# Two queue items per conv tile, and the value's weights requested as soon as the gate's unit runs

## The chip, the cores and the metric

The kernel runs on one core of one Trainium2 chip. The metric is the device time of one execution in microseconds; what is given is the median of several runs on one chip. The core has TensorE (PE in the profile, with its weight loads as PEld), VectorE (DVE), ScalarE (ACT), GpSimd (POOL) and SyncE (SP), which here only issues DMAs.

## The reference

Two layers run over 512 latent and 256 context tokens of width 1024. In each layer one input projection feeds three mixers, and a gated merge joins them; a gated feed-forward network follows.

```python
h = modulate(rms_norm(x)); a, na, qkv, og, dec, bet, mg = split(h @ w_in)
# A: a = [value | gate], 2 x 512 columns
y = value * sigmoid(gate); y = depthwise_conv31(y); ya = silu(layer_norm(y))
yb = neighbourhood_attention(norm(q), norm(k), v)        # from na, 3 x 512 columns
yc = gated_deltanet(qkv, dec, bet, og)                   # triangular solve per chunk, then a scan
x = x + m * (sum_b sigmoid(mg_b) * (y_b @ w_branch_b)) @ w_out
x = x + m' * conv_ffn(modulate(rms_norm(x)))
```

In the second layer the context tokens produce only keys and values, so their merge, feed-forward network and conv branch drop out.

## The kernel before

Every product with weights is done three times on split numbers: a weight tile of 128 x 1024 values arrives as `raw` by a DMA on SP's queue (L143, two buffers), ScalarE casts it to `whi` (L150, three buffers), VectorE takes the rest as `wlo` (L151, three buffers), and TensorE adds up whi x hi, whi x lo and wlo x hi. The function `wunit` does this for one tile.

The order of each engine's instructions is fixed before the run: the framework's scheduler places ready work, with the order of the program as its priority. Engines execute their own list strictly in order, and a buffer that is to be written again waits until its last reader is done.

The gated DeltaNet branch leaves TensorE much idle time: for each of two head pairs it builds a matrix E from decays, inverts its triangular blocks (`gdn_inverse`, whose off-diagonal 32 x 32 products write `iy`, `it` and `ir`, L986 to L999, after DMAs that gather `Td` and `E`), then scans the chunks, and ends in transposes `oT` (L933) copied to `oev` and stored. Between its steps the program calls `fill(us)`, which takes about that much TensorE work from `self.queue`, a queue of independent generators ("filler"). `fill` (L440 to L456) runs one generator at a time; when it starts one, it also advances the next one to its first yield, which is where the next one asks for its weights. So one item's weights are always requested one item ahead.

The queue holds, in this order: units of the neighbourhood attention's projection (`na_units`, L600 to L627: 36 units in layer 0 and 32 in layer 1; six units, or four, share one pair of weight tiles, which the first unit of such a set requests, so a set holds two of the three whi slots as long as it runs); among them the four conv tiles (`conv_a_proj`) at the places `CV_AT` gives; `na_finish`; and then 24 units of merge-gate projection (`mg_units`, L1036 to L1045), with the conv branch's layer norm between the last of them. A projection unit (`proj_gen`, L463 to L475) asks for its weights, yields, and then runs 24 matmuls per token stream: `pjl` for 512 latent tokens and, in layer 0, `pjc` for 256 context tokens. An na unit has 24 matmuls of 256 columns.

Places are `CV_AT = ((10, 12, 24, 36), (0, 10, 20, 30))`. In layer 0 sets have six units, so tile c0 stands inside the second set, c1 and c2 at the end of a set, and c3 behind the last. In layer 1 the sets have 4, 6, 6, 4, 6 and 6 units; c0 stands ahead of all, c1 and c2 at the end of a set, c3 inside the last.

A conv tile is one generator in the kernel before: gate projection, value projection, then tanh of the gate (ACT, L514), its product with the value (DVE, L515) and the store (L516). Only the gate's weights can be requested ahead; the value's are requested when the generator comes to its second `proj_gen`.

After the second head pair of a layer comes the attention (`attention`, L1055 and on): 12 loads of `ax` (10 in layer 1), transposes `aT` (L1071), loads of `vc` and `vl`, scores `sc` (L1121, L1122), the bias by DMA, row sums on VectorE (L1125), the normalised weights `P` (L1128) and their transposes `PT` (L1135). Beside this VectorE computes the conv branch's taps (L546). The rest of the filler is run up by a loop ahead of the merge (L434 to L437).

Of the kernel before, what the change touches and what calls it, by code (L numbers as in the profile page):

```python
# [9 lines left out]
F32 = mybir.dt.float32  # L10
F32R = mybir.dt.float32r
I32 = mybir.dt.int32
AF = mybir.ActivationFunctionType
ALU = mybir.AluOpType
# [50 lines left out]
class Net:  # L65
# [309 lines left out]
    def layer(self, l):  # L375
        nc, tc = self.nc, self.tc
        last = l == DEPTH - 1
        self.l, self.last = l, last
        dr = lambda n, sh: self.dr.tile(sh, F32, tag=n, name=n)
        self.d_ya, self.d_yc = dr("ya", [4, 128, NT]), dr("yc", [4, 128, NT])  # L380
        self.d_na = [dr(f"na{i}", [NT, 512]) for i in range(3)]
        self.d_sg, self.d_mg = dr("sg", [NT, 512]), dr("mg", [24, 128, NT])
        self.d_row = dr("row", [48, 128])
        self.d_ca, self.d_cy = dr("ca", [4, 128, NT]), dr("cy", [4, 128, NT])
        self.d_tok = {n: dr("tok" + n, [4, 128, 6, 128]) for n in "kv"}
        self.d_e = [dr(f"e{i}", [4, 24, 1024]) for i in range(3)]

        with ExitStack() as es:
            self.cp = es.enter_context(tc.tile_pool(name=f"cv{l}", bufs=1))
            with tc.tile_pool(name=f"head{l}", bufs=1) as self.hp:  # L390
                with tc.tile_pool(name=f"pre{l}", bufs=2) as self.ep:
                    self.km = self.hp.tile([128, 512], F32, name="km")
                    nc.sync.dma_start(self.km, self.A["km"])
                    self.og_proj()
                    self.gates()
                    self.gdn_proj()
                na, mg = self.na_units(), self.mg_units()
                cv = [self.conv_a_proj(i) for i in range(4)]
                ln = [self.conv_a_norm(t) for t in range(2 if last else 0, 6)]
                order = list(na)  # L400
                for i, p in enumerate(CV_AT[l]):
                    order.insert(i + p, cv[i])
                order.append(self.na_finish())
                for i, f in enumerate(mg):
                    order.append(f)
                    if len(mg) - i <= len(ln):
                        order.append(ln[len(ln) - len(mg) + i])
                self.queue = deque(order)
                self.live = None
                with tc.tile_pool(name=f"gdn{l}", bufs=1) as self.gp:  # L410
                    self.marks = []
                    for pr in range(2):
                        self.gdn_core(pr)
            while self.na_left:
                self.fill(0.1)
            taps = [f for c in range(4) for f in self.conv_a_taps(c)]
            self.open_zx()
            with tc.tile_pool(name=f"att{l}", bufs=2) as self.ap:
                self.attention(taps)
        with ExitStack() as es:  # L420
            if not last:
                self.dp = es.enter_context(tc.tile_pool(name="ada", bufs=2))
                self.ada_rows()
                self.todo = self.ada_steps(0, [*range(16, 24), *range(32, 40), *range(24, 32), *range(40, 48)]) + self.ada_steps(1, range(48))
            else:
                self.todo = []
            self.finish(l)
        if last:
            self.zes.close()
# [76 lines left out]

    def conv_a_proj(self, c):

        nc, l = self.nc, self.l
        ga = yield from self.proj_gen(self.A["w_b"][l, 4 + c], not self.last)  # L510
        aa = yield from self.proj_gen(self.A["w_b"][l, c], not self.last)
        for s, n in self.streams():
            th = self.tp.tile([128, 512], F32, tag="t1", name="th")
            nc.scalar.activation(th[:, :n], ga[s], AF.Tanh, scale=0.5)  # L514
            nc.vector.scalar_tensor_tensor(th[:, :n], th[:, :n], 1.0, aa[s], ALU.add, ALU.mult)  # L515
            nc.sync.dma_start(self.d_cy[c][:, self.sl(s)], th[:, :n])  # L516

    def conv_a_taps(self, c):

# [928 lines left out]
```

## Time and profile before

| | |
|---|---|
| median of three runs | 2603.09 us (2597.68 to 2608.0) |
| the profiled execution | 2592.68 us |
| its span | 2590.9 us |
| TensorE busy | 2495.3 us (96%) |
| VectorE busy | 1853.1 us (72%) |
| ScalarE busy | 1068.0 us (41%) |
| mean granted clock of TensorE | 0.983 |

The profile is one execution, with times from the start of its span. Waits are put down to the event that came last. Matmuls overlap in the array, so the cost of one in a run of them is read from start to start, not from the length that the row gives.

### The profile page before, as it was taken

To read this page: it belongs to the slowest core of one execution; us is meant where nothing else is said; L and a number is where in the kernel's file an instruction comes from. 1 tells how busy PE (TensorE), PEld (TensorE's weight loads), DVE (VectorE), ACT (ScalarE), POOL (GpSimd) and SP (SyncE) were. 2 spreads that over 40 slices of the span, in tenths; PEclk is the share of its full clock that TensorE was granted. 3 is DMA by queue.
4 is the path that set the end of the run, shared out by engine and by line. 5 is a ranking of instruction groups with operands and counts; after the bars stand their busy time and mean duration, and the time that the engine had idled before them with its cause. 6 is when DMAs were issued, how large, how long until landed. Compare 5 with 4: busy or idle time off the path is not lost. (4 is left out here: it accounts for less than half of the span.)

```text
span 2590.9 us, 42262 instructions
## 1 busy us (share of the span) xinstructions
PE 2495.3 (96%) x16079; PEld 2154.6 (83%) x16079; DVE 1853.1 (72%) x4138; ACT 1068.0 (41%) x2158; POOL 8.4 (0%) x32
## 2 busy tenths in 40 slices
PE   6999999999999999999999999998989999999999
PEld 3989898977778888888888898888877778988887
DVE  6676578799679988876656477776768977755463
ACT  3464343445342344223223355634344543533242
POOL 0000000000000000000000000000000000000000
PEclk8999999999999999999999989998999999999999
DMA  7223524353468554453442342343446375423332
GB/s 249 90 80 121 147 88 138 104 192 108 151 187 267 184 172 127 123 158 121 142 136 90 110 139 94 122 134 111 147 124 212 99 245 191 132 90 98 98 98 89
DMA packets 207275, 356.75 MB, mean 138 GB/s; under 512 B 54832, under 2 KB 103200, under 8 KB 206944
## 3 DMA queue, kind: packets, MB, share of 16 engines
q1 hardware_dynamic: 182176, 320.97, 39.4%
q10 hardware_dynamic: 24896, 33.09, 3.6%
q8 instruction: 126, 2.06, 0.3%
q14 instruction: 77, 0.63, 0.1%
HBM read 297.31 MB, written 56.68 MB: 137 GB/s over the span
## 5 line engine op out<-in xcount | busy, mean ns | idle before, releaser
L151 DVE TENSOR_TENSOR wlo<-raw,whi 128x1024 fp32r<-128x1024 f32 (+2 forms) x320 | 387.2, 1211 | 290.4 <-ACT whi L150 287.7
L150 ACT CAST whi<-raw 128x1024 fp32r<-128x1024 f32 (+2 forms) x320 | 332.6, 1040 | 605.4 <-PE dn L169 197.3
L169 PE MATMUL upl<-hl,whi 128*128 128x512 f32 (+1 forms) x728 | 282.1, 389 | 2.2 <-ACT whi L150 2.1
L169 PE MATMUL upl<-ol,whi 128*128 128x512 f32 (+1 forms) x728 | 281.7, 388 | 0.0
L169 PE MATMUL upl<-hl,wlo 128*128 128x512 f32 (+1 forms) x728 | 280.4, 386 | 0.2 <-DVE wlo L151 0.2
L546 DVE SCALAR_TENSOR_TENSOR ca<-yp,caw,ca 128x783 f32<-128x783 f32 (+1 forms) x240 | 213.6, 890 | 8.5 <-ACT ca L539 5.6
L475 PE MATMUL pjl<-hl,whi 128*128 128x512 f32 x512 | 211.1, 412 | 7.6 <-ACT whi L150 7.6
L475 PE MATMUL pjl<-ol,whi 128*128 128x512 f32 x512 | 206.6, 403 | 0.0
L475 PE MATMUL pjl<-hl,wlo 128*128 128x512 f32 x512 | 205.8, 402 | 0.3 <-DVE wlo L151 0.2
L169 PEld LDWEIGHTS upl<-hl,whi 128*128 128x128 f32 x728 | 136.7, 188 | 30.4 <-ACT whi L150 2.3
L169 PEld LDWEIGHTS upl<-ol,whi 128*128 128x128 f32 x728 | 136.8, 188 | 29.8
L169 PEld LDWEIGHTS upl<-hl,wlo 128*128 128x128 f32 x728 | 136.7, 188 | 29.7 <-DVE wlo L151 0.4
L169 PE MATMUL dn<-fll,whi 128*128 128x512 f32 x352 | 139.1, 395 | 0.0
L169 PE MATMUL dn<-fhl,wlo 128*128 128x512 f32 x352 | 139.0, 395 | 0.0
L169 PE MATMUL dn<-fhl,whi 128*128 128x512 f32 x352 | 138.6, 395 | 0.0
L475 PEld LDWEIGHTS pjl<-hl,whi 128*128 128x128 f32 x512 | 98.1, 192 | 29.1 <-ACT whi L150 9.7
L277 DVE CUSTOM_DVE_ANT_1 aj<-at,crows,par 128x512 f32<-128x512 f32 x128 | 93.2, 749 | 31.2 <-DMA at<-ada_t 19.1
L475 PEld LDWEIGHTS pjl<-hl,wlo 128*128 128x128 f32 x512 | 97.5, 191 | 21.5 <-DVE wlo L151 1.2
L475 PEld LDWEIGHTS pjl<-ol,whi 128*128 128x128 f32 x512 | 98.0, 191 | 18.8 <-issue 0.5
L611 PE MATMUL na<-wlo,hl 128*128 128x256 f32 x384 | 108.9, 284 | 0.6 <-DVE wlo L151 0.6
L611 PE MATMUL na<-whi,hl 128*128 128x256 f32 x384 | 109.2, 285 | 0.0
L611 PE MATMUL na<-whi,ol 128*128 128x256 f32 x384 | 109.2, 284 | 0.0
(392 smaller groups left out, 6464.7 us busy)
## 6 DMA issues: line engine op xcount, KB each, us to landing
raw<-w_b SPq DMA_DIRECT2D x88, 512.0 KB
raw<-f_up SPq DMA_DIRECT2D x88, 512.0 KB
at<-ada_t SPq DMA_DIRECT2D x160, 256.0 KB
raw<-w_o SPq DMA_DIRECT2D x32, 512.0 KB
raw<-f_dn SPq DMA_DIRECT2D x32, 448.0 KB
raw<-w_a SPq DMA_DIRECT2D x24, 512.0 KB
mg<-mge ACTq DMA_DIRECT2D x48, 256.0 KB
raw<-w_br SPq DMA_DIRECT2D x24, 512.0 KB
```

What stands on the lines that cost most here:

```text
L150: self.nc.scalar.copy(hi[:, :n], r[:, :n])
L151: self.split = self.nc.vector.tensor_sub(lo[:, :n], r[:, :n], hi[:, :n]).ins
L169: self.nc.tensor.matmul(o, wk[a], x[k][b], start=(k == 0 and i == 0), stop=(k == n - 1 and i == 2))
L277: V.tensor_tensor_reduce(p, w, self.crows[:, r, 4 * h:4 * h + 4], 1.0, m if h else self.p(l, "adab")[:, t:t + 1], ALU.mult, ALU.add, accum ...
L475: self.nc.tensor.matmul(o, wk[a], x[k][b], start=(k == 0 and i == 0), stop=(k == n - 1 and i == 2))
L546: nc.vector.scalar_tensor_tensor(a, y[:, k:k + n], w[:, 31 * c + k:31 * c + k + 1], a, ALU.mult, ALU.add)
L611: self.nc.tensor.matmul(ps[:, :256], x[k][a], wk[b], start=(k == 0 and j == 0), stop=(k == 7 and j == 2))
```

## The change

`conv_a_proj` returns two generators in place of one. The first, `gate()`, does the gate's projection and leaves its result in a dictionary; the second, `value()`, does the value's projection and what follows. Both are put in the queue next to each other, at the place where the tile stood. Since `fill` advances the next item when it starts one, the value's weights are now requested when the gate starts, and the weights of what follows the tile when the value starts. The number of instructions of every kind stays the same. Six lines are added above the lines behind this function, so L986 of before is L992 after, and so on.

```diff
--- before.py
+++ after.py
@@ -399,7 +399,7 @@
                 ln = [self.conv_a_norm(t) for t in range(2 if last else 0, 6)]
                 order = list(na)
                 for i, p in enumerate(CV_AT[l]):
-                    order.insert(i + p, cv[i])
+                    order[2 * i + p:2 * i + p] = cv[i]
                 order.append(self.na_finish())
                 for i, f in enumerate(mg):
                     order.append(f)
@@ -506,14 +506,20 @@
 
     def conv_a_proj(self, c):
 
-        nc, l = self.nc, self.l
-        ga = yield from self.proj_gen(self.A["w_b"][l, 4 + c], not self.last)
-        aa = yield from self.proj_gen(self.A["w_b"][l, c], not self.last)
-        for s, n in self.streams():
-            th = self.tp.tile([128, 512], F32, tag="t1", name="th")
-            nc.scalar.activation(th[:, :n], ga[s], AF.Tanh, scale=0.5)
-            nc.vector.scalar_tensor_tensor(th[:, :n], th[:, :n], 1.0, aa[s], ALU.add, ALU.mult)
-            nc.sync.dma_start(self.d_cy[c][:, self.sl(s)], th[:, :n])
+        nc, l, st = self.nc, self.l, {}
+
+        def gate():
+            st["g"] = yield from self.proj_gen(self.A["w_b"][l, 4 + c], not self.last)
+
+        def value():
+            aa = yield from self.proj_gen(self.A["w_b"][l, c], not self.last)
+            for s, n in self.streams():
+                th = self.tp.tile([128, 512], F32, tag="t1", name="th")
+                nc.scalar.activation(th[:, :n], st["g"][s], AF.Tanh, scale=0.5)
+                nc.vector.scalar_tensor_tensor(th[:, :n], th[:, :n], 1.0, aa[s], ALU.add, ALU.mult)
+                nc.sync.dma_start(self.d_cy[c][:, self.sl(s)], th[:, :n])
+
+        return gate(), value()
 
     def conv_a_taps(self, c):
```

The scheduler makes new lists from this. On SP, around tile c1 of layer 0, before (`raw_2888` is the gate's load, `raw_3134` from w_b the value's, `raw_2925` and `raw_2931` from w_a the next na pair's; `cy` is tile c0's store):

```order
L143 DMA raw_2888<-w_b 128x1024
L948 DMA e0_407<-E_2226 32x24x32 x4
L143 DMA raw_2925<-w_a 128x1024
L949 DMA Eb_2520<-e0_407 48x1x1024
L950 DMA Tf_2522<-e0_407 48x1x1024
L952 DMA Tt_2521<-eye32 112x1024
L516 DMA cy_404<-th_2849 128x512
L516 DMA cy_404<-th_2853 128x256
L143 DMA raw_2931<-w_a 128x1024
L143 DMA raw_3134<-w_b 128x1024
```

and of the change, where `raw_2925` from w_b is the value's load and `raw_3128` and `raw_3134` the na pair's:

```order
L143 DMA raw_2888<-w_b 128x1024
L954 DMA e0_407<-E_2226 32x24x32 x4
L143 DMA raw_2925<-w_b 128x1024
L955 DMA Eb_2520<-e0_407 48x1x1024
L956 DMA Tf_2522<-e0_407 48x1x1024
L958 DMA Tt_2521<-eye32 112x1024
L520 DMA cy_404<-th_2849 128x512
L520 DMA cy_404<-th_2853 128x256
L143 DMA raw_3128<-w_a 128x1024
L143 DMA raw_3134<-w_a 128x1024
```

The value's load has moved ahead of both loads of the na pair, and ahead of c0's store.

On TensorE, at the inverse of layer 1's first head pair, before (`iy` are the 48 inverse products, a projection runs right ahead of them):

```order
L475 MATMUL pjl<-hl_15251,whi 128x512
L475 MATMUL pjl<-ol_15252,whi 128x512
L475 MATMUL pjl<-hl_15251,wlo 128x512
L986 MATMUL iy<-Td,E 32x32 x48
L997 MATMUL it<-Y,E 32x32
L999 MATMUL ir<-E,Y 32x32 x3
```

and of the change, at the second and third of those products:

```order
L617 MATMUL na<-whi,hl_15243 128x256
L617 MATMUL na<-wlo,hl_15243 128x256
L617 MATMUL na<-whi,ol_15244 128x256
L617 MATMUL na<-whi,hl_15245 128x256
L992 MATMUL iy<-Td,E 32x32 x2
L617 MATMUL na<-wlo,hl_15245 128x256
L617 MATMUL na<-whi,ol_15246 128x256
```

Na units that stood behind the inverse have moved ahead of it and between its products. Counted over this list, 24 pjl and 144 na matmuls more stand ahead of the last `iy` of that pair; in layer 0, 47 pjl and 46 pjc more stand ahead of the last `iy` of the second pair.

On TensorE, at the start of layer 1's attention, before (`aT` are transposes of `ax`, and the projections between them belong to merge-gate units):

```order
L475 MATMUL pjl<-hl_15245,wlo 128x512
L1071 MATMUL aT<-kc,ax 128x128 x8
L475 MATMUL pjl<-hl_15247,whi 128x512
L1071 MATMUL aT<-kc,ax 128x128 x8
L475 MATMUL pjl<-ol_15248,whi 128x512
L475 MATMUL pjl<-hl_15247,wlo 128x512
L1071 MATMUL aT<-kc,ax 128x128 x4
L475 MATMUL pjl<-hl_15249,whi 128x512
L475 MATMUL pjl<-ol_15250,whi 128x512
L475 MATMUL pjl<-hl_15249,wlo 128x512
L1071 MATMUL aT<-kc,ax 128x128 x4
```

and of the change:

```order
L475 MATMUL pjl<-ol_15252,whi 128x512
L475 MATMUL pjl<-hl_15251,wlo 128x512
L1077 MATMUL aT<-kc,ax 128x128 x40
L1127 MATMUL sc<-akT,aqT 128x256
L1128 MATMUL sc<-akT,aqT 128x256
L1127 MATMUL sc<-akT,aqT 128x256
L1128 MATMUL sc<-akT,aqT 128x256
L1127 MATMUL sc<-akT,aqT 128x256
```

The transposes stand in one run with the score products behind them; the projections that lay between them have moved ahead. Ahead of the first `oT` of the second head pair there are 97 pjl matmuls more than before in layer 1, and 51 pjl and 51 pjc more in layer 0; ahead of the attention's first `PT` 18 pjl more in layer 1, and 8 pjl and 9 pjc more in layer 0. TensorE's list is the same up to the place of c1 in layer 0, from the attention of layer 0 to the start of layer 1's filler, and from the attention of layer 1 to the end.

## Rows read from the trace of the kernel before

**Rows 1.** Page, part 1: engine, busy us, share of the span, instructions.
```profile
PE 2495.3 (96%) x16079; PEld 2154.6 (83%) x16079; DVE 1853.1 (72%) x4138; ACT 1068.0 (41%) x2158; POOL 8.4 (0%) x32
```

**Rows 2.** Waits of TensorE: engine, line, waited for, us in total, times, longest.
```profile
PE iy L986 <- DMA Td<-e: 10.7, 5, 4.0
...
PE pjl L475 <- ACT whi L150: 7.6, 5, 2.6
```

**Rows 3.** Timeline of TensorE at three conv tiles: start, length, instruction, [idle before].
```profile
271.32 0.50 PE L475 MATMUL pjl<-hl,whi 128*128 128x512 f32 x1 [0.79 <-ACT whi L150]
...
361.92 0.50 PE L475 MATMUL pjl<-hl,whi 128*128 128x512 f32 x1 [2.59 <-ACT whi L150]
...
1708.46 0.79 PE L475 MATMUL pjl<-hl,whi 128*128 128x512 f32 x1 [2.56 <-ACT whi L150]
```

**Rows 4.** Timeline of ScalarE at two conv tiles of layer 1.
```profile
1706.42 1.04 ACT L150 CAST whi<-raw 128x1024 fp32r<-128x1024 f32 x1
...
1840.92 1.04 ACT L150 CAST whi<-raw 128x1024 fp32r<-128x1024 f32 x1 [4.87 <-PE pjl L475]
```

**Rows 5.** Windows: stretch, us, busy and instructions per engine, PEclk, DMA share, GB/s.
```profile
363.40:367.00 3.60, 3.60 (x19) 3.60 (x19) 3.60 (x20) 0.85 (x1) 0.00 (x0) 0.53 0.00 0
1708.00:1716.00 8.00, 7.31 (x18) 5.32 (x19) 5.89 (x16) 0.40 (x1) 0.00 (x0) 0.57 0.46 156
1756.00:1774.00 18.00, 11.48 (x345) 10.52 (x344) 4.78 (x9) 7.08 (x16) 0.00 (x0) 0.53 0.63 180
```

**Rows 6.** Timeline of TensorE at the inverses of three head pairs.
```profile
445.90 0.24 PE L986 MATMUL iy<-Td,E 32*32 32x32 f32 x2 [1.42 <-DMA Td<-e]
...
1755.87 0.22 PE L986 MATMUL iy<-Td,E 32*32 32x32 f32 x2 [3.14 <-DMA Td<-e]
...
1757.33 0.32 PE L986 MATMUL iy<-Td,E 32*32 32x32 f32 x4 [1.24 <-DMA Td<-e]
...
1758.51 0.70 PE L986 MATMUL iy<-Td,E 32*32 32x32 f32 x36 [0.86 <-DMA Td<-e]
...
1891.77 0.24 PE L986 MATMUL iy<-Td,E 32*32 32x32 f32 x2 [4.02 <-DMA Td<-e]
```

**Rows 7.** Timeline of TensorE, layer 1: projection and na matmuls in a row.
```profile
1717.26 0.39 PE L475 MATMUL pjl<-hl,wlo 128*128 128x512 f32 x1
1717.48 0.28 PE L611 MATMUL na<-whi,hc 128*128 128x256 f32 x1
1717.60 0.28 PE L611 MATMUL na<-wlo,hc 128*128 128x256 f32 x1
```

**Rows 8.** Timeline between scan and attention of each layer: ends and waits, three engines.
```profile
509.39 0.38 PE L933 MATMUL oT<-kc,sgr 128*128 128x128 f32 x2
...
515.08 1.04 ACT L539 ACTIVATE ca<-yp,par,caw 128x783 f32<-128x783 f32 x1 [3.89 <-DMA yp<-cy]
...
549.66 0.49 DVE L1125 CUSTOM_DVE_ANT_0 sc<-sc,bias,m 128x256 f32<-128x256 f32 x1 [3.00 <-DMA bias<-bias]
...
552.10 0.41 PE L1135 MATMUL PT<-kc,P 128*128 128x128 f32 x2 [2.59 <-DVE ls L1127]
...
1957.27 0.32 PE L933 MATMUL oT<-kc,sgr 128*128 128x128 f32 x1
...
1989.23 0.49 DVE L1125 CUSTOM_DVE_ANT_0 sc<-sc,bias,m 128x256 f32<-128x256 f32 x1 [5.44 <-DMA bias<-bias]
...
1991.46 0.32 PE L1135 MATMUL PT<-kc,P 128*128 128x128 f32 x1 [4.79 <-DVE P L1128]
```

**Rows 9.** Windows over the same two stretches; columns as in rows 5.
```profile
509.40:552.10 42.70, 37.66 (x225) 32.31 (x224) 33.40 (x61) 16.74 (x35) 0.00 (x0) 0.96 0.71 246
1957.30:1991.50 34.20, 28.96 (x155) 22.65 (x155) 23.54 (x48) 12.94 (x26) 0.16 (x2) 1.00 0.73 249
```

**Rows 10.** These windows, line 475 alone: PE busy, PEld busy, PEclk, DMA share, GB/s.
```profile
509.40:552.10 42.70, 30.48 (x149) 23.49 (x148) 0.96 0.71 246
1957.30:1991.50 34.20, 23.76 (x90) 16.18 (x89) 1.00 0.73 249
```

## The prediction

> **What bounds the kernel now.** I read the page's busy times first. TensorE is busy for 2495.3 of 2590.9 us [rows 1], so all its idle time together is 95.6 us, and no change of order can win more than that and what a halved clock costs. So the time is TensorE's instruction stream, which runs in order: the end moves by what is added to or taken from TensorE's idle time and from its time at half clock, and by nothing else. VectorE, at 1853.1 us, is second and has room.
>
> Next came the view of waits. The change aims at the wait of the projections' matmuls (pjl, L475) for ScalarE's cast of the weights (whi, L150): 7.6 us in five places, 2.6 the longest [rows 2]. Beside it stands a wait of 10.7 us in five places of the triangular inverse's first product (iy, L986) for a DMA; it has nothing to do with weights, but the filler stands right ahead of it.
>
> Then I looked up each conv tile on the timeline. Three of them stop TensorE between gate and value: c1 in layer 0 for 0.79 us, c2 in layer 0 for 2.59, c1 in layer 1 for 2.56 [rows 3]. ScalarE shows the reason. At c1 of layer 1 the casts start at 1706.42, after the gate's last matmul has gone; at c3 of layer 1 the cast starts at 1840.92, straight after it, the engine having idled 4.87 us for that matmul [rows 4]. The value's weights need a whi slot. There are three: the gate has one, the next two units' pair, requested ahead, has the others.
>
> The granted clock was next: it is at 0.53 over the 3.6 us behind the wait of c2 and at 0.57 over the 8 us behind the wait of c1 in layer 1, where the level in force for most of the time is 1.2 GHz in place of 2.4 [rows 5]. So these waits cost more than their own length.
>
> Last I looked at places where TensorE idles for something that no weight order can hasten: the iy products of each head pair [rows 6], and the stretch from the scan's last transposes (oT, L933) to the attention's first softmax (PT, L1135) in each layer, whose rows come with their reckoning below. These decide the forecast.
>
> **The waits and the clock at the tiles.** At c1 and c2 of layer 0 and c1 of layer 1 the tile stands where one set of neighbourhood-attention (na) units ends, so the previous pair's slots are free when the gate starts and the value's cast can run beside the gate's matmuls. That takes out 0.79 + 2.59 + 2.56 = 5.9 us. The clock stays up behind c2 (3.6 us at 0.53: 3.6 x 0.47 = 1.7) and behind c1 of layer 1 (8 us at 0.57: 8 x 0.43 = 3.4), together 5.1 us. At tiles inside a set (c0 of layer 0, c3 of layer 1) two slots stay with the set and the gate has the third; the value's cast goes on starting after the gate's last matmul, as at 1840.92 [rows 4]. I count nothing there. The weights' bytes, casts and matmuls stay the same in number; SP's queue only passes the value's load ahead of the na pair's, as its order shows, and it waits on nothing new there that TensorE needs before.
>
> **The inverse's wait.** Counted in the order of TensorE's instructions, more filler stands ahead of the last iy product of layer 0's second pair (47 pjl and 46 pjc matmuls more) and of layer 1's first pair (24 pjl and 144 na). From start to start a pjl costs 0.22 us and an na matmul of 256 columns 0.12 [rows 7]; a pjc has 256 columns too, so it gets 0.12. That is 47 x 0.22 + 46 x 0.12 = 15.9 and 24 x 0.22 + 144 x 0.12 = 22.6 us. The waits of 1.42 us at 445.90 and of 3.14 + 1.24 + 0.86 us from 1755.87 on [rows 6] are then filled by useful work: 6.7 us. Between 1756 and 1774 the clock stood at 0.53 with TensorE busy 11.48 us [rows 5]; at full clock that would cost at most 11.48 x 0.47 = 5.4 less. The products there are small and partly paced by other things, so between 0 and 5.4 I take half, 2.7. The 4.02 us of layer 1's second pair [rows 6] stay, for its E data start from the end of the scan before, which comes no sooner.
>
> Gains so far: 5.9 + 5.1 + 6.7 + 2.7 = 20.4 us. If nothing were given back, the profiled execution of 2592.68 us would be 2572.
>
> **What is given back.** The filler that now runs ahead is the same filler that before lay behind the scan. From the first oT to the first PT TensorE has little of its own to do: the chain goes through ScalarE's copies and the DMAs (a tap waits to 515.08 for its yp, the row sums at 549.66 and 1989.23 for the bias, with idle times of 3.00 and 5.44 us), and it takes 42.7 us in layer 0 (509.39 to 552.10) and 34.2 in layer 1 (1957.27 to 1991.46) [rows 8]. TensorE was nevertheless busy for 37.66 and 28.96 us of it [rows 9], and 30.48 and 23.76 of that were merge-gate projections (L475) [rows 10]. So the filler covered it, and TensorE idled only 5.0 and 5.2 us.
>
> In the new order 51 pjl and 51 pjc more stand ahead of layer 0's first oT of that pair, and 8 and 9 more ahead of the first PT: 43 and 42 have left the stretch, 43 x 0.22 + 42 x 0.12 = 14.5 us of cover. In layer 1 it is 97 pjl more ahead of the oT and 18 ahead of the PT: 79 x 0.22 = 17.4 us. The order of layer 1 shows it plainly: ten times four transposes (aT) and four score products in one run with no projection between them. If the chain keeps its length, TensorE idles 19.5 and 22.6 us there, and 14.5 + 17.4 = 31.9 us come back.
>
> The unknown is the chain's length. No row shows it without filler. It can shrink by what filler costs it: the DMA share is 0.71 and 0.73 there [rows 9], and the bias, whose DMA shares the queue with raw loads, was late by 3.00 and 5.44 us, 8.4 in all. At the other end it keeps its length and TensorE's work after a long idle stretch runs at half clock, worth the 1.7 us that the clock cost behind c2, once in each layer: +3.4. Between -8.4 and +3.4 I take -2, near the middle, since the bias is asked for behind other loads of the attention that stay.
>
> Sum: -20.4 + 31.9 - 2 = +9.5 us. On the profiled execution that gives 2602. The runs shown have a median of 2603.09, 10.4 above that execution, so I predict 2613 us for the median.
>
> **A rule against the trace.** At the tiles the rows show that a stretch behind a wait ran at 0.53 and 0.57 of the clock [rows 5]. The Trainium skill, "TensorE: Matmul & The Clock Gate", section "Loop structure matters more than you think", says to lay the loop out so that matmuls follow one another and transfers run beside them, since an engine that waits long for a DMA runs cold afterwards. By that rule the change is right at the tiles and wrong at the two stretches before the attention, where it removes the matmuls that lay beside the DMAs. The trace agrees at the tiles (0.53 and 0.57); no row shows the two stretches without filler, and the sum does not change by it. The Trainium skill, "Perfetto Trace Analysis", section "Optimization Strategies", makes keeping the matmul engine busy the goal, and by that alone the 20.4 us would be gain: that is the first rival, and only the order behind the tiles speaks against it.
>
> **The rivals.**
> The gain is kept. The chains before the attention get shorter by what filler takes from them, or the scheduler's order matters less than the DMAs' timing, so that the idle time does not appear. With all kept, -20.4 us: 2583; with half of the cover's loss, -20.4 + 16 = -4: 2599. For it: the bias' waits, and a DMA share of 0.7 that falls without filler. Against it: the loss is longer than all that the chain could win (31.9 against 8.4).
>
> The attention's start is late (slower). Mechanism: in each layer the scan starts only when the in-order stream has worked off the filler ahead of it (15.9 and 22.6 us), and the chain behind the scan runs uncovered. The forecast lies 3.5 us under the bound of slower, so it decides from the point where 3.5 of the 9.4 us that the inverse's waits and clock were to give do not come; with none of 6.7 + 2.7 kept and the chain 2 us longer through the cold clock, the sum is -11.0 + 31.9 + 2 = +23: 2626.
>
> The value's weights come no sooner. If the extra request finds no slot at the set's ends either, the 11.0 us at the tiles stay; with the moved filler the sum is -9.4 + 31.9 - 2 = +20: 2623. With no move either it is no change, 2603. Against it: at the set's end the previous pair is done before the gate starts.
>
> **How the numbers follow.** About 0.5% (13 us) is what a measurement of this kernel can tell from no change: below 2590 is faster, above 2616 slower. The forecast (+3 to +16) has 0.45, of which 0.36 lies within the band and 0.09 above it; the kept gain 0.25, 0.17 of it beyond 0.5% and 0.08 within; the late start 0.24, nearly all slower; the weights not sooner 0.06, half of it slower. So faster 0.17, same 0.47, slower 0.36. The forecast's own range is 2606 to 2619; the 8-in-10 range takes in most of the late start and half of the kept gain: 2588 to 2632.
>
> **What would show it.** The wait of pjl for whi should fall from 7.6 us to about 2, with no half clock behind c2 and behind c1 of layer 1. The iy wait should fall from 10.7 to about 4. In the two stretches TensorE's idle time should rise from 5.0 and 5.2 to about 20 and 23 us, with the wait for the softmax (PT) much longer than now. The prediction fails if those stretches shrink by more than 10 us together, or if the scan's own waits move: it takes them as they are.

## The result and the profile after

The changed kernel takes 2625.88 us in the median of seven runs (2614.82 to 2635.65), against 2603.09 for the kernel before (2596.25 to 2611.24, seven runs). The ratio is 1.0096, with an interval of 1.0073 to 1.0118: it is slower by 0.73 to 1.18%, 19 to 31 us. The profiled executions have spans of 2616.8 and 2590.9 us, 25.9 apart.

The page of the change, part 1 (busy us, share of the span, instructions):

```profile
PE 2498.3 (95%) x16079; PEld 2157.1 (82%) x16079; DVE 1853.3 (71%) x4138; ACT 1066.6 (41%) x2158; POOL 8.6 (0%) x32
```

Against [rows 1] TensorE is busy 3.0 us longer with the same 16079 instructions, and its idle time has grown from 95.6 to 2616.8 - 2498.3 = 118.5 us, by 22.9. So 22.9 of the 25.9 us are idle time. The other 3.0 are busy time of the same instructions, some of them at a lower clock (0.980 in the mean, where it was 0.983).

The waits of TensorE (total us, times, longest):

```profile
PE PT L1141 <- DVE ls L1133: 16.4, 3, 8.3
...
PE iy L992 <- DMA Td<-e: 10.2, 3, 5.0
...
PE aT L1077 <- DMA ax<-na: 9.0, 1, 9.0
...
PE aT L1077 <- DVE ax L1074: 5.9, 1, 5.9
...
PE pjl L475 <- ACT whi L150: 1.7, 2, 0.9
```

The wait of pjl for whi has fallen from 7.6 to 1.7 us [rows 2]: the change does what it says. The wait for Td has hardly moved, from 10.7 to 10.2 us, and the waits ahead of the attention (PT for the row sums' DVE work, aT for the loads of ax) have come up: 16.4 + 9.0 + 5.9 us.

The same waits on the timeline, each with its idle time:

```profile
455.50 0.31 PE L992 MATMUL iy<-Td,E 32*32 32x32 f32 x2 [5.05 <-DMA Td<-e]
...
546.49 0.45 PE L1077 MATMUL aT<-kc,ax 128*128 128x128 f32 x1 [5.95 <-DVE ax L1074]
...
568.11 0.45 PE L1141 MATMUL PT<-kc,P 128*128 128x128 f32 x1 [7.84 <-DVE ls L1133]
...
1775.21 0.22 PE L992 MATMUL iy<-Td,E 32*32 32x32 f32 x2 [0.91 <-DMA Td<-e]
...
1918.13 0.26 PE L992 MATMUL iy<-Td,E 32*32 32x32 f32 x1 [4.25 <-DMA Td<-e]
...
1997.77 0.44 PE L1077 MATMUL aT<-kc,ax 128*128 128x128 f32 x1 [8.95 <-DMA ax<-na]
...
2017.84 0.45 PE L1141 MATMUL PT<-kc,P 128*128 128x128 f32 x1 [8.29 <-DVE ls L1133]
```

These answer to [rows 6] and [rows 8]. In layer 0's second pair the wait for Td has grown from 1.42 to 5.05 us. In layer 1's first pair it has fallen from 3.14 (with two more behind it) to 0.91, and in the second it stands at 4.25 against 4.02. Each stretch between scan and attention now has two long waits, one ahead of the transposes and one ahead of PT.

Windows over the change's counterparts: the inverse of layer 0's second pair, its stretch between scan and attention, layer 1 from c1 to the first iy, the iy products of its first pair, and layer 1's stretch (columns as in [rows 5]; a stretch runs from the first oT to the first PT):

```profile
455.50:470.90 15.40, 15.39 (x164) 13.11 (x164) 5.91 (x6) 2.90 (x6) 0.00 (x0) 0.85 0.55 138
528.20:568.10 39.90, 23.43 (x140) 19.72 (x139) 33.09 (x61) 15.17 (x32) 0.00 (x0) 0.84 0.71 236
1717.40:1775.20 57.80, 56.90 (x386) 52.71 (x386) 42.11 (x90) 19.77 (x31) 0.00 (x0) 1.00 0.45 142
1775.20:1788.10 12.90, 12.89 (x191) 12.55 (x191) 1.69 (x5) 4.62 (x14) 0.00 (x0) 1.00 0.66 171
1985.40:2017.80 32.40, 13.45 (x74) 10.57 (x74) 23.14 (x53) 10.28 (x23) 0.16 (x2) 0.77 0.72 245
```

and of the kernel before, for those that [rows 9] doesn't hold:

```profile
445.90:450.40 4.50, 4.50 (x115) 3.84 (x115) 4.36 (x5) 2.02 (x4) 0.00 (x0) 1.00 1.06 202
1700.30:1755.90 55.60, 49.09 (x315) 44.03 (x314) 40.10 (x87) 18.12 (x28) 0.00 (x0) 0.94 0.45 136
1755.90:1759.70 3.80, 1.70 (x94) 1.45 (x95) 0.00 (x0) 1.79 (x4) 0.00 (x0) 0.53 1.05 189
```

The stretches before the attention are shorter by 2.8 and 1.8 us (39.9 and 32.4 against 42.7 and 34.2), but TensorE is busy for 23.43 and 13.45 us of them in place of 37.66 and 28.96: idle 16.5 and 19.0 us where it was 5.0 and 5.2. The granted clock in them is 0.84 and 0.77, where it was 0.96 and 1.00. From the first to the last iy of layer 0's second pair it now takes 15.4 us in place of 4.5, with filler between the products and the clock at 0.85; in layer 1's first pair 12.9 in place of 3.8. TensorE is busy for nearly all of both (15.39 and 12.89 us), so this is useful work, but work that had covered something else. And layer 1 from c1 to the first iy takes 57.8 us in place of 55.6, busy for 56.90 in place of 49.09 us.

### The profile page after: what moved, and what is told of

Read it like the earlier page. It is cut to its first block, busy times and chain, and to the rows that moved or that the text cites. A ratio compares the mean times of both kernels' runs of the same rounds, so it can differ in the third digit from the quotient of the medians.

```text
span 2616.8 us, 42284 instructions
## 1 busy us (share of the span) xinstructions
PE 2498.3 (95%) x16079; PEld 2157.1 (82%) x16079; DVE 1853.3 (71%) x4138; ACT 1066.6 (41%) x2158; POOL 8.6 (0%) x32
## 4 chain that ended last, share of the span: by engine, by line
PE 68%; DVE 9%; DMA 9%; issue 2%; ACT 2%; SPq 0%; ACTq 0%; DVEq 0%; POOL 0%; POOLq 0%
PE upl L169 19%; PE dn L169 10%; PE pjl L475 7%; PE upc L169 5%; PE na L617 4%; PE mbl L169 4%; PE pjl L169 3%; DVE ca L552 2%; PE wo L169 2%; PE pjc L475 2%; DVE wlo L151 1%; PE og L179 1%; PE mbc L169 1%; DMA e<-Tf 1%; DMA at<-ada_t 1%
## 5 line engine op out<-in xcount | busy, mean ns | idle before, releaser
L169 PEld LDWEIGHTS upl<-hl,whi 128*128 128x128 f32 x728 | 136.7, 188 | 31.9 <-ACT whi L150 2.4
```

The lines of the kernel that those rows point to most:

```text
L169: self.nc.tensor.matmul(o, wk[a], x[k][b], start=(k == 0 and i == 0), stop=(k == n - 1 and i == 2))
```

## The experiments

Eleven kernels ran, each with the kernel before on the same chip. A few of them use one small tool: a block under `issue_after(x)` queues what it emits on x's engine behind x, without a wait. `last_iy` is the last iy product (L992) of the latest inverse, `last_ot` the last oT transpose.

**Filler put back, and its control.** The first is the change with three groups of filler queued behind the iy products of the pair before:

```diff
-        self.fill(FILL[l]["x"])
+        with self.tc.issue_after(self.last_iy):
+            self.fill(FILL[l]["x"])
...
-                self.fill(FILL[self.l]["pre"])
+                with self.tc.issue_after(self.last_iy):
+                    self.fill(FILL[self.l]["pre"])
...
-                self.fill(FILL[self.l]["e"])
+                with self.tc.issue_after(self.last_iy) if l and pr else ExitStack():
+                    self.fill(FILL[self.l]["e"])
```

(This diff and those below show the main lines alone, some with their conditions written more plainly than in the kernel.)

> The change, with its early filler put back: on TensorE the filler of the attention's first fills (x and pre) is queued behind the last iy product of the layer's second head pair, and in layer 1 the filler of the second pair's e fills behind the last iy of the first pair. No work is left out. Theory A (the loss is the cover that left the stretch between scan and attention, with the scan starting later behind extra filler): TensorE's idle time in the two stretches goes back from 16.5 and 19 us to 5 to 9 each, the waits at the conv tiles stay gone, and the kernel is 5 to 18 us faster than before (2585 to 2598 against 2603). Theory B (the loss comes from the early loads and casts of the value's weights themselves, which stand in SP's and VectorE's queues ahead of the inverse): the filler's place is of no matter, and the kernel stays 15 to 25 us slower than before.

The second has the same edit in the kernel before.

> The kernel before, with the same three groups of filler queued behind the same iy products; the order of TensorE differs from before's only in layer 0, by 12 to 15 pjl and pjc, from the second inverse to the first softmax. It is the control of the run beside it: theory A and B both expect before within 5 us (2598 to 2608); if it is faster by as much as the run beside it, the holds and not the conv tiles are what gains.

Measured: 2603.71 us against 2597.01, ratio 1.0030 (1.0018 to 1.0043), and 2601.59, ratio 1.0024 (1.0008 to 1.0040). So with the filler back 0.66 of the 0.96% are gone, about 17 of 25 us: most of the loss is where the filler stands. But it did not become faster than before, which theory A had expected, and its control is nearly as slow: the holds alone cost the kernel before 0.24%, about 6 us and a little more than the 5 allowed. Between two kernels with the same holds the two-item tiles cost 0.06%, which is nothing that can be measured, and win nothing either.

The windows of the first one's two stretches and its wait for Td:

```profile
518.50:560.60 42.10, 36.24 (x225) 30.28 (x226) 35.14 (x64) 17.03 (x36) 0.00 (x0) 0.97 0.75 248
...
1973.20:2007.10 33.90, 27.13 (x145) 21.44 (x146) 25.32 (x55) 13.02 (x27) 0.16 (x2) 0.97 0.74 250
...
PE iy L993 <- DMA Td<-e: 24.2, 7, 12.0
```

The cover is back: idle 42.1 - 36.24 = 5.9 and 33.9 - 27.13 = 6.8 us. But the wait for Td is 24.2 us in all, and half of it is one wait in layer 0:

```profile
456.35 0.31 PE L993 MATMUL iy<-Td,E 32*32 32x32 f32 x2 [12.04 <-DMA Td<-e]
```

The control waits much less for Td, in all and in layer 0's second pair:

```profile
PE iy L987 <- DMA Td<-e: 16.4, 7, 5.2
...
450.41 0.24 PE L987 MATMUL iy<-Td,E 32*32 32x32 f32 x2 [2.79 <-DMA Td<-e]
```

In layer 0 the two have the same order from this inverse on, and the tiles c1 and c2 cost nothing in the first. Yet its iy comes 5.9 us later (456.35 against 450.41). What was won at c1 and c2 is lost in front of iy, because the inverse itself is late: with the two waits behind it, TensorE waits 14.4 us for Td there, and 5.2 in the control.

**One layer alone.** The edit makes one item of the two in the other layer:

```diff
-        return gate(), value()
+        return (gate(), value()) if l == 0 else (both(),)     # both() runs the one, then the other
```

> The change in layer 0 alone; in layer 1 each conv tile stays one item. Theory A: the loss of each layer is its own, 14.5 us of cover and the late iy in layer 0 less 5 us at the tiles, and the trace of the change has the end of layer 0's attention 16 us late: +12 to +18 us. Theory B: layer 0's inverse is late because two raw loads stand ahead of its own loads on SP: also +12 to +18, since both lie in this layer; the runs with filler back tell these apart.

> The change in layer 1 alone; in layer 0 each conv tile stays one item. Theory A: the layer loses 17.4 us of cover and wins 11 to 14 us of waits and clock: +4 to +10 us, and with the run beside it the sum is the change's +23 to +26. If the layers are not additive, something they share (the state in which layer 1 starts) is at work.

Measured: 2610.97, ratio 1.0070 (1.0046 to 1.0094), and 2611.10, ratio 1.0049 (1.0028 to 1.0070). In us of 2597 that is +18 and +13, against expected +12 to +18 and +4 to +10 (by the medians alone both are +14). Each layer loses by itself, and the sum, 1.19%, lies near the change's 0.96%; the intervals overlap. Layer 1 loses more than I allowed it, though its interval, 7 to 18 us, reaches into what I allowed. Theory B for layer 0 expected the same as theory A, so this run does not tell them apart.

**One tile alone.** Only c2 of layer 0 is two items.

```diff
-        return gate(), value()
+        return (gate(), value()) if (l, c) == (0, 2) else (both(),)
```

> One tile alone, c2 of layer 0, becomes two items; all others stay one. The order of TensorE then has the same early filler in layer 0 as the change has (45 pjl and 44 pjc more ahead of the last iy of the second pair against 47 and 46). Theory A (the loss of layer 0 is the early filler and the late inverse that come with c2's request, not the number of tiles changed): as slow as the change in layer 0 alone, +12 to +20 us. Theory B (each tile's own loads and casts add to it): a third of that, +3 to +8 us.

Measured: 2611.84 against 2598.88, ratio 1.0051 (1.0033 to 1.0068), +13 us: theory A. One tile's request, which takes 2.59 us of wait away, moves nearly all the filler of the layer and costs most of its loss. Its DMA queue on SP looks like the change's, shown next: the inverse's load Eb goes out 12.1 us after the last stores of E began (402.99 and 390.89).

**The inverse's loads on a queue of their own.** Before, Eb goes out 4.6 us after the last stores of E began:

```profile
386.30 2.12 SPq L948 DMA_DIRECT2D e<-E  x4
...
389.22 0.35 SPq L143 DMA_DIRECT2D raw<-w_b  x1
...
390.85 0.66 SPq L949 DMA_DIRECT2D Eb<-e  x1
```

In the change two raw loads stand between. Each goes out as VectorE ends the split that reads its buffer's old tile (395.69 and 398.77), so Eb goes out 12.0 us after the stores, and VectorE waits 7.02 us for the load behind it, Tf:

```profile
387.68 2.12 SPq L954 DMA_DIRECT2D e<-E  x4
...
395.71 3.43 SPq L143 DMA_DIRECT2D raw<-w_b  x2
...
399.68 0.66 SPq L955 DMA_DIRECT2D Eb<-e  x1
...
407.96 0.69 DVE L957 COPY Eb<-Tf 48x1024 f32<-48x1024 f32 x1 [7.02 <-DMA Tf<-e]
```

From these loads on, the inverse is a chain of steps on VectorE (Tm, Tt), then stores, and then the loads of Td. Its first step, its last one and the first load of Td, before:

```profile
403.38 0.19 DVE L958 TENSOR_TENSOR Tm<-Eb,Tt 112x31 f32<-112x31 f32 x1
...
430.44 0.19 DVE L960 TENSOR_TENSOR Tt<-Tt,Tm 112x31 f32<-112x31 f32 x1
...
443.72 0.88 SPq L975 DMA_DIRECT2D Td<-e  x2
```

and of the change:

```profile
409.49 0.19 DVE L964 TENSOR_TENSOR Tm<-Eb,Tt 112x31 f32<-112x31 f32 x1 [0.84 <-DMA Tt<-eye]
...
437.38 0.19 DVE L966 TENSOR_TENSOR Tt<-Tt,Tm 112x31 f32<-112x31 f32 x1
...
452.68 0.88 SPq L981 DMA_DIRECT2D Td<-e  x2
```

So Td goes out 9.0 us later. Of this, 1.4 us are there when the stores of E begin, 4.7 come from there to the first step (17.1 us before, 21.8 now), 0.8 within the steps (27.1 and 27.9, with four weight splits between them in place of three), and 2.0 between the last step and Td (13.3 and 15.3).

Three kernels put the loads Eb, Tf and Tt on GpSimd's queue:

```diff
-        nc.sync.dma_start(Eb[0:48], de[:, 0:12, :])
-        nc.sync.dma_start(Tf[64:112], de[:, 12:24, :])
+        lq = nc.gpsimd if self.l == 0 else nc.sync
+        lq.dma_start(Eb[0:48], de[:, 0:12, :])
+        lq.dma_start(Tf[64:112], de[:, 12:24, :])
...
-        nc.sync.dma_start(Tt[0:112], self.A["eye32"][0:112])
+        lq.dma_start(Tt[0:112], self.A["eye32"][0:112])
```

> The change with its early filler put back, as in the first run of the series, and the inverse's three loads of layer 0 (Eb, Tf, Tt) issued on GpSimd's queue in place of SP's, where two raw weight loads stand ahead of them and wait for a raw buffer. Theory A (what is left of the loss, 7.8 us, is layer 0's inverse: its Td wait is 14.4 us with filler back, and its loads go out behind those raw loads): the Td wait falls to 2 to 5 us, and the time falls by 8 to 12 us, to between 6 us faster than before and equal. Theory B (the wait comes from VectorE, which splits more weight tiles inside the inverse's chain): the Td wait falls by less than 3 us and the time stays 5 to 8 us over before.

> The kernel before with the inverse's three loads of layer 0 on GpSimd's queue; TensorE's order differs by one or two matmuls. Control of the two beside it. Theory A: in before only one raw load in layer 0's first pair stands ahead of them in the way, so within 4 us of before. Theory B: the same. If it is faster by more, the queue is a gain of its own and must be taken off the two beside it.

> The change with the inverse's three loads of layer 0 on GpSimd's queue and its order of filler as it is. Theory A: the 5.05 us wait for Td in layer 0 and the half clock behind it go (together 5 to 8 us), but the late scan and the uncovered stretches stay: +15 to +20 us over before. Theory B: no change against the change, +23 to +26.

Measured: with filler back 2604.93 against 2599.99, ratio 1.0025 (1.0009 to 1.0040); before 1.0007 (0.9991 to 1.0023); the change 2619.43, ratio 1.0084 (1.0063 to 1.0106). Of the first:

```profile
393.51 2.12 SPq L955 DMA_DIRECT2D e<-E  x4
...
399.45 0.61 POOL L957 DMA_DIRECT2D Eb<-e  x1 [14.78 <-DMA e<-E]
...
408.89 0.19 DVE L966 TENSOR_TENSOR Tm<-Eb,Tt 112x31 f32<-112x31 f32 x1 [1.57 <-DMA na<-ev]
...
415.10 1.23 DVE L151 TENSOR_TENSOR wlo<-raw,whi 128x1024 fp32r<-128x1024 f32 x1 [2.31 <-ACT whi L150]
...
439.52 0.19 DVE L968 TENSOR_TENSOR Tt<-Tt,Tm 112x31 f32<-112x31 f32 x1
...
PE iy L994 <- DMA Td<-e: 23.1, 7, 12.1
```

The load now goes out 5.9 us after the stores began and no longer waits for a raw buffer, and still the wait for Td is 23.1 us in place of 24.2 (and 4.6 us more of iy's waiting are put down to the load of E). Theory A of this experiment has fallen: SP's queue is not alone in making the inverse late. The time from the stores of E to the first step did fall, from 21.6 to 15.4 us, but two other things took the 6.2 us back. The stores of E themselves began 3.5 us later in this run (393.51 against 389.97 with SP's queue), for a cause that I did not find. And the steps took 30.6 us in place of 27.9 (in the run with SP's queue they go from 411.52 to 439.40), because VectorE's list has weight splits between them, and two of these now waited 2.31 and 0.24 us for ScalarE's cast of their tile. The third kernel shows the same against the change: 15.6 in place of 21.8 us to the first step, stores 3.7 us later, 30.4 us of steps. Theory B's number came true, but not its reason: the one extra split makes the steps only 0.8 us longer. So the inverse is tied to the filler's weights twice, on SP's queue and in VectorE's list. The third kernel's +22 us (16 to 28) lies between the two theories and does not decide; its wait for Td in layer 0 is 4.01 us in place of 5.05.

**Filler held behind the scan.** The change with the later pre fills queued behind the last oT:

```diff
-                self.fill(FILL[self.l]["pre"])
+                held -= 1            # starts at 7 in layer 0 and 4 in layer 1
+                with self.tc.issue_after(self.last_ot) if held < 0 else ExitStack():
+                    self.fill(FILL[self.l]["pre"])
```

> The change, with the last 5 of the attention's 12 pre fills in layer 0 and the last 6 of 10 in layer 1 queued on TensorE behind the second pair's last oT, so that as much filler covers the stretch between scan and attention as before, while the inverse is still late by the filler ahead of it (15.8 us in layer 0 and 22 in layer 1 by the order). Theory A in its simple form (the cover that left that stretch is the loss): TensorE's idle time there goes back to 5 to 9 us in each layer and the kernel is within 8 us of before. Theory C (the cover is only moved, since the scan then lacks it: 16 us in layer 0 and 20 in layer 1): the idle time turns up inside the scan, and the kernel stays 15 to 30 us slower than before.

Measured: 2631.37 against 2599.99, ratio 1.0127 (1.0105 to 1.0150), +33 us: theory C, and a little past its upper end. TensorE at the second pair's first oT in both layers, and the windows of the stretch behind it:

```profile
525.87 0.48 PE L939 MATMUL oT<-kc,sgr 128*128 128x128 f32 x1 [14.53 <-DVE sgr L933]
...
1985.73 0.74 PE L939 MATMUL oT<-kc,sgr 128*128 128x128 f32 x2 [12.06 <-DVE sgr L933]
...
525.90:570.20 44.30, 36.36 (x215) 30.15 (x216) 34.45 (x64) 17.60 (x36) 0.00 (x0) 0.92 0.68 219
...
1985.70:2021.60 35.90, 29.16 (x145) 22.50 (x146) 23.25 (x47) 12.86 (x26) 0.16 (x2) 0.88 0.66 221
```

Behind the scan TensorE is covered again (44.3 - 36.36 = 7.9 and 35.9 - 29.16 = 6.7 us idle), but at the end of the scan it waits 14.53 and 12.06 us for VectorE. The scan is hardly shorter for having 16 and 20 us less filler: from the last iy to the first oT it takes 54.6 us in layer 0 and 50.0 in layer 1, in the change 57.3 and 53.5. So there is one supply of filler for three places that need it, the wait ahead of iy, the scan and the stretch behind it; what one gets too early the others lack.

**What follows from it: a version between.** In layer 0 only c1 is two items, since its request moves no filler behind the first pair; in layer 1 all four are, with the holds of the first experiment. The two kernels differ in how much of the second pair's e filler is held:

```diff
-        return gate(), value()
+        return (gate(), value()) if l or c == 1 else (both(),)
...
-                self.fill(FILL[self.l]["e"])
+                with self.tc.issue_after(self.last_iy) if l and pr else ExitStack():          # the first
+                with self.tc.issue_after(self.last_iy) if l and pr and hh else ExitStack():   # the second
+                    self.fill(FILL[self.l]["e"])
```

> Two items for c1 of layer 0 (whose request moves no filler behind the first pair) and for all four tiles of layer 1; in layer 1 the filler of the second pair's e fills and of the attention's x and pre fills is queued behind the iy products of the pair before it, so that 24 pjl and 21 na in place of 24 and 144 stand early. Theory A: layer 0 is as before less 0.8 us, layer 1 keeps its 6 us at c1 and gives back little: 1 to 6 us faster than before. Theory D (what is won at a tile is lost at the next wait for the DMA of Td, since the inverse's chain sets when the scan starts): equal to before within 3 us.

> As the run beside it, but of the second pair's e fills only those of the second head are held, so that TensorE has 24 pjl and 99 na early ahead of layer 1's first inverse and the wait for Td there is filled. Theory A: the cover between scan and attention is the same as beside it, so equal within 3 us. Theory E (filler ahead of the iy is worth its length in the Td wait of 7.6 us that stood there with all held): 3 to 7 us faster than the run beside it.

Measured: 2600.29 against 2598.88, ratio 1.0004 (0.9988 to 1.0020), equal to before, so theory D; and 2593.99, ratio 0.9977 (0.9961 to 0.9993), faster than before by 0.07 to 0.39% and than the run beside it by 6 us, so theory E. Layer 1's first inverse in the first:

```profile
1763.89 0.28 PE L998 MATMUL iy<-Td,E 32*32 32x32 f32 x2 [5.20 <-DMA Td<-e]
...
1765.57 0.31 PE L998 MATMUL iy<-Td,E 32*32 32x32 f32 x4 [1.41 <-DMA Td<-e]
```

and in the second:

```profile
1771.43 0.22 PE L998 MATMUL iy<-Td,E 32*32 32x32 f32 x2 [1.41 <-DMA Td<-e]
```

With 78 na matmuls more ahead of the last iy, waits of 5.20 + 1.41 us (and 0.80 behind them) have become one of 1.41. By the two ratios this version is 1.2% faster than the change. Against the kernel before its gain is small, and its interval ends close to 1.

## Why the prediction was right or wrong

The direction, the places and the 8-in-10 range (2588 to 2632) were right. The size was not: 2613 was forecast and 2625.88 came; +9.5 us against +25.9 in the profiles. The result lies outside the forecast's own range (2606 to 2619), and the case I held likeliest, a result within 0.5%, did not happen. The wide range held because it took in the second rival, a late start of the attention. That rival's 2626 agrees with the result in part by luck: as it said, the inverse's waits gave next to nothing, but it also had the chain 2 us longer, where it became 4.6 us shorter, and none of the inverse's clock gained, where some 3 us were.

**The tiles: right.** 5.9 us of waits were to go, and 7.6 - 1.7 = 5.9 went. The tiles inside a set kept theirs.

**The cover: right in kind, a fourth too large.** I expected 31.9 us more idle time in the two stretches; it is (16.5 - 5.0) + (19.0 - 5.2) = 25.3. The chain shrank by 2.8 + 1.8 = 4.6 us without filler; I had allowed it 8.4 at most and taken 2 with the clock.

**The inverse's wait: wrong.** "The waits of 1.42 us at 445.90 and of 3.14 + 1.24 + 0.86 us from 1755.87 on [rows 6] are then filled by useful work: 6.7 us." In layer 1 they were (5.24 to 0.91). In layer 0 the wait grew to 5.05 us, though by the order 22 pjl and 22 pjc more (7.5 us) stood ahead of its first iy, because Td itself came 9.0 us later (SP issues its first load at 452.68 in place of 443.72). In all the wait fell by 0.5 us, so 6.2 of the 6.7 us did not come. The step took the inverse's chain as fixed and counted only TensorE against it; the same filler asks SP for raw loads and VectorE for splits, and both serve the inverse. The sentence on SP's queue ("it waits on nothing new there that TensorE needs before") looked only at c1, where it holds; at c2 the queue before the second pair's loads is the one shown above.

**The clock: right where I credited it, and its price elsewhere too small.** I credited 5.1 us at the tiles and 2.7 at the inverse, 7.8 in all, so TensorE's busy time had to fall by that; it rose by 3.0, a miss of 10.8 us. The credits themselves came: in the change the clock is at 1.00 behind c2 and behind c1 of layer 1, and layer 1's first inverse has 4.15 us of busy time at half clock (from 1791.2 to 1798.1) in place of 10.68. The price is at the stretches before the attention. The times at 1.2 GHz there and just behind the first PT, before:

```profile
530.70:534.20 3.50, 3.50 (x17) 3.17 (x16) 3.50 (x6) 2.12 (x4) 0.00 (x0) 0.51 1.00 330
1991.60:1995.10 3.50, 3.31 (x12) 2.64 (x12) 3.24 (x9) 2.76 (x7) 0.00 (x0) 0.51 0.84 274
```

and of the change:

```profile
545.40:552.30 6.90, 5.50 (x25) 4.96 (x26) 6.18 (x11) 2.55 (x4) 0.00 (x0) 0.51 1.02 360
562.40:572.80 10.40, 4.38 (x20) 2.89 (x22) 8.06 (x22) 4.00 (x10) 0.00 (x0) 0.51 0.43 132
1992.60:2002.90 10.30, 5.11 (x23) 4.74 (x24) 9.02 (x17) 2.48 (x5) 0.16 (x2) 0.50 0.94 334
2013.10:2023.40 10.30, 5.56 (x32) 4.35 (x32) 7.79 (x25) 4.67 (x11) 0.00 (x0) 0.50 0.36 115
```

TensorE is busy at that level for 20.55 us where it was 6.81; as an estimate, half of the difference, 6.9 us, is what this costs. In each stretch the clock falls at each of the two long waits shown with the result, before the wait is over. The forecast named this price at 3.4 us and then folded it into a shorter chain, so that it stood at nothing in the sum. Half clock at layer 1's second pair costs another 2.4 us by the same estimate (6.27 and 5.52 us of busy time from 1917.5 and 1934.6 on, in place of 3.50 and 3.50). The granted clock does not explain the last 1.5 us of the miss. The Trainium skill, "TensorE: Matmul & The Clock Gate", section "Loop structure matters more than you think", says that an engine with long waits for DMAs between its matmuls runs cold. The trace now agrees at the two stretches too (0.84 and 0.77 over the whole of them, where it was 0.96 and 1.00), though three of their four long waits end with work of VectorE and not with a DMA.

With the idle time the forecast was close: -5.9 - 6.7 + 31.9 = +19.3 against +22.9, but in part because errors cancel: the cover came out 6.6 us smaller, the inverse's wait gave 6.2 us less, and some 4 us of idle time are at places that the forecast did not count. Of the 16.4 us between +9.5 and +25.9, 3.6 are idle time, 10.8 busy time, and 2 the shorter chain, which the forecast took off the idle time and which is already in the 22.9.

**The cause, as far as it is shown.** That the early filler is the main cause is shown by the first two experiments: with it held, about 17 of 25 us come back with the two-item tiles still there, and the control, which has the same holds and one-item tiles, is as slow within 0.06%. The kernel with c2 alone shows how little it takes. That the filler is a supply which three places share is shown by the hold behind the scan. Of the 8 us that do not come back, the control has 6 by the holds alone; what the traces add is that the 3.4 us saved at layer 0's tiles are given back in front of its late inverse (14.4 us of waiting for Td there against 5.2 in the control). Why that inverse is late is read from the timelines and not shown by a run: in the change 4.7 of its 9.0 us lie between the stores of E and the first step, where the two raw loads stand on SP's queue. No run brought it back: the one with the queue cleared lost the gain again to later stores and to VectorE's splits. The 2.0 us between its last step and Td stay open.

## What to carry to other kernels

Where a scheduler orders independent filler around a serial chain, a wait taken out of the filler can move all the filler behind it, as it did here: before counting the wait as gain, count in the new order how much filler stands ahead of each point where the chain is slow by itself, and what that point had before. A stretch that was hidden by filler costs most of what the filler covered when the filler runs early (here 25.3 of 31.9 us), and the clock with it. If a wait is to go, hold the filler in its place and look whether the chain's own transfers and casts still come first.

## What the runs showed that I had not expected

One request, for the weights of one tile (c2 of layer 0), moved 45 pjl and 44 pjc matmuls across an inverse and cost 13 us to save 2.59. The scan got only 2.7 and 3.5 us shorter when it lost its filler: 14.53 and 12.06 us of its filler's time came back as waiting at its end. The steps of a serial chain on VectorE took 2.8 us longer when the chain started earlier, because weight splits stand between them in VectorE's fixed order and waited for their casts. And a stretch of DMAs in series lost only 2.8 of 42.7 and 1.8 of 34.2 us when most of the filler that ran beside it was gone (43 of 74 pjl in layer 0, 79 of 89 in layer 1), at nearly the same DMA share (0.71 and 0.72 against 0.71 and 0.73).
